# Transposing the seven MLP input forms on the way into DRAM instead of on the way out

## The chip, the cores and the metric

The kernel runs one layer of a streaming encoder on one core of a Trainium2 chip. The metric is device microseconds (us) of that core, from one launch. Five engines work side by side, each through its own instruction stream in order: TensorE (PE in the profile; its weight loads are PEld), VectorE (DVE), ScalarE (ACT), GpSimd (POOL) and SyncE (SP). SP does no arithmetic here: it issues DMAs, and so does POOL. A DMA that an engine issues waits in that engine's stream until its data are ready, and what stands behind it waits too. Engines signal each other by semaphores.

## The reference, cut to what matters

One layer, 2048 frames of 1024 features, everything in float32:

```
h = layer_norm(ALPHA * h + mix, ln1_g, ln1_b)        # mix: mLSTM and gated linear attention heads
xa = memory_cross_attention(h, mem, x_wq, x_wk, x_wv, x_wo)
h = layer_norm(ALPHA * h + xa, ln2_g, ln2_b)
ff = squared_relu_mlp(h, w_ff1, w_ff2)               # square(relu(h @ w_ff1)) @ w_ff2, width 4096
h = layer_norm(ALPHA * h + ff, ln3_g, ln3_b)
```

The kernel keeps float32 accuracy by splitting each factor into a high and a low float16 half, and multiplying high by high, high by low and low by high (`mm3`, lines 167 to 172).

## The kernel before, in words

The kernel has three stages. Stage A (to about 1130 us of the span) computes the mixer. Stage B (about 1130 to 1730 us) goes over 16 tiles of 128 frames with three steps that are staggered in one loop: in its turn i it runs `s1(i)` (output projection of the mixer and the first layer norm, LN1), `s2(i-1)` (attention scores and softmax) and `s3(i-2)` (attention output and the second layer norm, LN2). Stage C (to the end) is the MLP.

TensorE multiplies along the partition axis, so every left operand must stand transposed. Stage B has that done by transposing DMAs that SP issues (`to_T`, line 222): for each tile, the mixer's output `y_d` into `whi`, LN1's output into `wlo` (`h1T` in the code) and the softmax into `pT`. `pT` has one buffer, so tile i's transpose waits until `s3(i-1)` has read the last one.

The MLP's first product uses a fast matrix scheme with 7 products in place of 8: two neighbouring tiles and the two halves of the features make a 2x2 block of the input, and 7 combinations of its four parts (the forms, 128x512 each) are multiplied by 7 combinations of the weights. The forms of a pair are made at the end of `s3(i)` for odd i (i is then the pair's second tile; lines 978 to 998): GpSimd and VectorE make the sums, and four turns of a loop make the halves of forms k = 0 and 1, of 2, of 3 and 4, and of 5 and 6 in a tile `hs3` (two buffers; `hs` in the profile). A turn's ACT copy makes the high half, its DVE subtraction the low half, and GpSimd stores the result to `h2_d`, one DRAM tile per pair (`h_d` in the profile, which leaves numbers out of names; the other `h_d` that is loaded into `r` is the mixer's residual). Then the tile itself is scaled and stored (`ah_d`).

The MLP goes over the frames in two halves of 8 tiles, and in each half over 16 weight groups. Stage C needs form f of a half as one tile [128, 4 pairs, 2, 4, 128], transposed: `c_form` reads it from `h2_d` by four transposing DMAs of 256 KB, one per pair. For the first half, SP issues 7x4 of them at turn 16 of stage B, as soon as the memory of LN1's weights is free; the first product block, `ffn1(0, 0)`, stands between `s3(14)` and `s3(15)` on TensorE. For the second half they are issued in the last weight group of the first half. `ffn1(j, half)` has 7 products of 12 matmuls, in the order A11, S2, S3, S1, A12, S4, A22, into two banks of each of two PSUM names (`mm`, `o`); ACT copies A11 out, DVE adds the others up.

The tiles `whi` and `wlo` of pool `wsp` have four buffers each. Weights pass through them in stages A and C, `h1T` in stage B.

What sets the order: within an engine, a scheduler orders the instructions of stages A and B before the run, by its own model of durations, and the chip keeps that order; in stage C most of it is in the order of the code. Two instructions of POOL matter below. The power of LN1 and LN2 (`L202`, 1/sqrt by `pow`) is on the way of every layer norm. And between a `partition_all_reduce` (`L130`) and the next ordinary instruction POOL loads other code, and again on the way back.

Of the kernel before, what the change touches and what calls it, by code (L numbers as in the profile page):

```python
# [10 lines left out]
F16 = mybir.dt.float16  # L11
# [6 lines left out]
P = 128  # L18
T = 2048
D = 1024  # L20
KC = D // P
NT = T // P
# [37 lines left out]
def layer_kernel(ctx: ExitStack, tc, a, out):  # L60
    nc = tc.nc
# [5 lines left out]
    wsp = ctx.enter_context(tc.tile_pool(name="wsp", bufs=4))  # L67
    big = ctx.enter_context(tc.tile_pool(name="big", bufs=4))
    ps = ctx.enter_context(tc.tile_pool(name="ps", bufs=1, space=PSUM))
    dram = ctx.enter_context(tc.tile_pool(name="dram", bufs=1, space=bass.MemoryType.DRAM))  # L70
# [4 lines left out]
    def ps_s():  # L75
        return ps.tile([P, 512], F32, name="s", bufs=4)
# [4 lines left out]
    def slab(shape, dt):  # L81
        return big.tile(shape, dt, name="slab")
# [6 lines left out]
    h0_d = [dram.tile([P, D], F32, name=f"h0_d{i}") for i in range(NT)]  # L89
    ah2_d = [dram.tile([P, D], F32, name=f"ah2_d{i}") for i in range(NT)]  # L90
    y_d = [dram.tile([CPB, P, 8, 2, P], F16, name=f"y_d{b}") for b in range(NB)]
    h2_d = [dram.tile([P, 7, D], F16, name=f"h2_d{i}") for i in range(NT // 2)]
    w1_d = [dram.tile([4, P, 2048], F16, name=f"w1_d{j}") for j in range(NJ)]
    w2_d = [dram.tile([2, P, 2048], F16, name=f"w2_d{j}") for j in range(NJ)]
    nm_d = dram.tile([64, P], F32, name="nm_d")
# [71 lines left out]
    def mm3(psum, pairs, start=True, stop=True):  # L167
        n = len(pairs)
        for i, (lh, ll, rh, rl) in enumerate(pairs):
            nc.tensor.matmul(psum, lhsT=lh, rhs=rh, start=(start and i == 0), stop=False)  # L170
            nc.tensor.matmul(psum, lhsT=lh, rhs=rl, start=False, stop=False)  # L171
            nc.tensor.matmul(psum, lhsT=ll, rhs=rh, start=False, stop=(stop and i == n - 1))  # L172
# [21 lines left out]
    def layer_norm(x, gt, bt, spread=False):  # L194
        st = sm.tile([P, 2, 6], F32, name="st")
        mv = sm.tile([P, 2], F32, name="mv")
        rs = sm.tile([P, 2], F32, name="rs")
        for i in range(2):
            nc.vector.bn_stats(st[:, i, :], x[:, i * 512:(i + 1) * 512])  # L199
        nc.vector.bn_aggr(mv, st.rearrange("p a b -> p (a b)"))  # L200
        nc.vector.tensor_scalar(rs[:, 0:1], mv[:, 1:2], EPS, None, ALU.add)
        nc.gpsimd.tensor_tensor(rs[:, 1:2], rs[:, 0:1], mhalf[:, 0:1], ALU.pow)  # L202
        if spread:
            nm = sm.tile([P, 1], F32, name="amx")
            nc.vector.scalar_tensor_tensor(nm, mv[:, 0:1], -1.0, rs[:, 1:2], ALU.mult, ALU.mult)
            nc.scalar.activation(x, x, AF.Identity, scale=rs[:, 1:2], bias=nm)
            nc.gpsimd.tensor_tensor(x, x, gt, ALU.mult)
            nc.gpsimd.tensor_tensor(x, x, bt, ALU.add)
            return
        nc.vector.scalar_tensor_tensor(x, x, mv[:, 0:1], gt, ALU.subtract, ALU.mult)  # L210
        nc.vector.scalar_tensor_tensor(x, x, rs[:, 1:2], bt, ALU.mult, ALU.add)
# [9 lines left out]
    def to_T(dst, src):  # L221
        nc.sync.dma_start_transpose(dst, src)  # L222
# [696 lines left out]
    with ExitStack() as bctx:  # L919
# [45 lines left out]
        def s3(i):  # L965
            r, pT = rs_.pop(i)[0], es_.pop(i)
            for n in range(2):
                ns = slice(n * 512, (n + 1) * 512)
                po = ps_s()
                mm3(po, [(pT[:, 0, f * P:(f + 1) * P], pT[:, 1, f * P:(f + 1) * P], vo[f // 2][0][:, f % 2, ns],  # L970
                          vo[f // 2][1][:, f % 2, ns]) for f in range(8)])
                nc.vector.scalar_tensor_tensor(r[:, ns], po, inv_o, r[:, ns], ALU.mult, ALU.add)
            layer_norm(r, g2, b2)
            if i % 2 == 0:
                even[0] = r
                return
            r0, r1 = even[0], r
            if i < NT - 1:
                fm = wst.tile([P, 2048], F32, name="stg")
                fm = fm[:, 0:D], fm[:, D:2 * D]  # L980
            else:
                fm = [rr.tile([P, D], F32, name="r") for _ in range(2)]
            t1, t2, t3, t4 = (f[:, k * 512:(k + 1) * 512] for f in fm for k in range(2))
            a0, a1, c0, c1_ = r0[:, 0:512], r0[:, 512:D], r1[:, 0:512], r1[:, 512:D]
            nc.gpsimd.tensor_tensor(t1, c0, a0, ALU.subtract)
            nc.gpsimd.tensor_tensor(t3, c1_, c0, ALU.subtract)
            nc.vector.tensor_tensor(t2, c1_, t1, ALU.subtract)
            nc.vector.tensor_tensor(t4, a1, t2, ALU.subtract)
            for k, src in ((0, r0), (2, c1_), (3, fm[0]), (5, fm[1])):
                n = src.shape[-1] // 512  # L990
                hs = bx.tile([P, 2, 2, 512], F16, name="hs3", bufs=2)[:, 0:n]
                src = src.rearrange("p (n c) -> p n c", n=n)
                nc.scalar.copy(hs[:, :, 0], src)
                nc.vector.tensor_tensor(hs[:, :, 1], src, hs[:, :, 0], ALU.subtract)
                nc.gpsimd.dma_start(h2_d[i // 2][:, k:k + n], hs.rearrange("p n s c -> p n (s c)"))
            for ii, rx in ((i - 1, r0), (i, r1)):
                nc.scalar.activation(rx, rx, AF.Copy, scale=ai_h2)
                nc.gpsimd.dma_start(ah2_d[ii], rx)
# [5 lines left out]
        ORDER = (0, 4, 5, 3, 1, 2, 6)  # L1004

        def c_form(t, half, f):
            for p in range(4):
                to_T(t[:, p].rearrange("p s k t -> p (s k) t"), h2_d[half * 4 + p][:, f])
            forms[half, f] = t

        def form_tile(pool, name):
# [169 lines left out]
        for i in range(2, NT + 2):  # L1181
            if i < NT:
                s1(i, bx)
            if i == NT:
                b2ctx.close()
                c1 = c1ctx.enter_context(tc.tile_pool(name="c1", bufs=1, reuse_waits="tile", side="right"))
                for f in ORDER[:5]:
                    c_form(form_tile(c1, f"hf{f}"), 0, f)
# [4 lines left out]
            if i == NT:  # L1193
                za, zb = slab([P, 4096], F32), slab([P, 4096], F32)
                stgs[1] = za[:, 0:2048]
                zt += [za[:, 2048 + k * 512:2560 + k * 512] for k in range(4)]
                for n, f in enumerate(ORDER[5:]):
                    c_form(form_stage(zb[:, n * 2048:(n + 1) * 2048]), 0, f)
                w1_load(1)
# [3 lines left out]
            if i == NT + 1:  # L1203
                mx_0 = ffn1(0, 0, {})
            s3(i - 2)
            if i == NT - 2:
                stgs[0] = wst.tile([P, 2048], F32, name="stg")
                w1_new(0)
                w1_load(0)
                t = w1_tasks(0, stgs[0])  # L1210
# [4 lines left out]
    with ExitStack() as cctx:  # L1215
# [3 lines left out]
        for n in range(2):  # L1219
            t = slab([P, 4, D], F32)  # L1220
# [63 lines left out]
        with tc.manual_schedule():  # L1284
# [17 lines left out]
            n = 0  # L1302
            slots = None
            for half in range(2):
                for j in range(NJ):
# [4 lines left out]
                    if half == 0:  # L1310
                        w2t[j] = [w2s[n % 2][:, k] for k in range(2)]
                        t2 = w2_tasks(j)
                        if j + 1 < NJ:
                            w1_new(j + 1)
                            t1 = w1_tasks(j + 1, stgs[1])
                            t1["bound"]()
                            t1["scale"]()
                            ta = t20 if j == 1 else t2
                            ex = {0: [t1["split_a"], t1["split_b"], ta["bound"]],
                                  1: [t1["sums_a"], ta["scale"], t1["sums_b"], t1["split_s"]],  # L1320
                                  2: [lambda: t1["split_l"](0)], 3: [ta["split"]],
                                  4: [lambda: t1["split_l"](1)]}
                            if j == 1:
                                ex[3].append(u0[5])
                        else:
                            w1_reload(0)
                            slots = [forms[0, f] for f in ORDER[:4]]
                            slots = [spare, form_stage(stgs[1]), slots[0], form_stage(stgs[0])] + slots[1:]
                            ex = {0: [lambda: c_form(slots[1], 1, ORDER[1]), t2["bound"], t2["scale"]],
                                  1: [t2["split"], lambda: c_form(slots[2], 1, ORDER[2])]}  # L1330
                            for k in range(3, 7):
                                ex[k - 1] = [lambda k=k: c_form(slots[k], 1, ORDER[k])]
# [38 lines left out]
                    if half == 0 and j == NJ - 1:  # L1371
                        accs[:] = [*accs[8:10]]
                        for f in ORDER[4:]:
                            t = forms[0, f].rearrange("p i s k t -> p (i s k t)").bitcast(F32)
# [87 lines left out]
```

## Time and profile before

| what | value |
|---|---|
| median of 3 runs | 3002.34 us (3002.3 to 3006.09) |
| the profiled execution | 3002.87 us, of which the span is 3001.0 us |
| granted TensorE clock, mean | 0.951 |
| busy, share of the span | PE 91%, DVE 66%, ACT 37%, POOL 15% |
| transposing DMAs that read the forms back | 56, of 256 KB each |

A row of the timeline gives start, duration and engine of an instruction, its line, operation and tiles, and in brackets how long the engine was idle before it and what ended that. PE's durations overlap, since matmuls are pipelined: neighbouring 512-column matmuls start 0.22 us apart at the full clock (1.0, 2.4 GHz) and 0.43 us apart at half of it. SPq and POOLq rows are DMA issues, and last as long as the issue, not the transfer.

### The profile page before, as it was taken

The page shows a single profiled execution, that of the slowest core. Times are in us where ns is not written, and L with a number is a line of the kernel's source. Part 1 is how long each engine was busy: PE and PEld are TensorE (multiplying, and loading weights), DVE is VectorE, ACT ScalarE, POOL GpSimd, SP SyncE. Part 2 cuts the span into 40 slices and gives each one's busy share as a digit, 9 for nine tenths or more (in the row PEclk, how much of TensorE's full clock was granted, in tenths as well). Part 3 has the DMA queues.
Part 4 walks back from the last instruction along what each step waited for, and adds up shares of the span by engine and source line. Part 5 has one row for each costly group of instructions (what it writes and reads, how often), then busy time and mean ns, then how long its engine had stood idle before and what let it go on. Part 6 is the DMA issues. An engine that isn't in the chain of part 4 may idle for free.

```text
span 3001.0 us, 41124 instructions
## 1 busy us (share of the span) xinstructions
PE 2738.2 (91%) x16282; PEld 1545.8 (52%) x16282; DVE 1991.3 (66%) x3774; ACT 1096.3 (37%) x1715; POOL 447.6 (15%) x573
## 2 busy tenths in 40 slices
PE   3679989989998898999999779999999999999997
PEld 2346667666665665565565334444444444444443
DVE  8956774655768666676666467777776676555547
ACT  3335444434444543233223254444443222222230
POOL 1102113322433221121111110000000000000003
PEclk8789999988989999999999889999999999999999
DMA  7832331010001335344435963333345522122211
GB/s 240 240 118 86 106 97 38 20 42 9 23 26 62 98 120 128 66 133 106 109 102 134 175 216 142 134 134 134 134 146 141 194 90 109 67 77 78 78 53 57
DMA packets 276993, 319.51 MB, mean 106 GB/s; under 512 B 200944, under 2 KB 217856, under 8 KB 268096
## 3 DMA queue, kind: packets, MB, share of 16 engines
q1 hardware_dynamic: 268096, 285.43, 31.3%
q0 software_dynamic: 8704, 31.46, 2.9%
q8 instruction: 127, 2.08, 0.3%
q14 instruction: 66, 0.54, 0.1%
HBM read 165.58 MB, written 102.96 MB: 89 GB/s over the span
## 4 chain that ended last, share of the span: by engine, by line
PE 67%; DVE 15%; issue 7%; POOL 4%; ACT 3%; DMA 2%; SPq 2%; POOLq 0%; ACTq 0%; DVEq 0%
PE s L170 9%; PE s L171 9%; PE s L172 9%; PE mm L170 9%; PE mm L172 8%; PE mm L171 8%; PE o L172 4%; PE o L170 4%; PE o L171 4%; SPq L222 2%; DVE wmx L114 1%; DVE qk L334 1%; DVE wlo L148 1%; DVE st L199 1%; PE o L651 1%
## 5 line engine op out<-in xcount | busy, mean ns | idle before, releaser
L1245 DVE SCALAR_TENSOR_TENSOR slab<-s,uiv,slab 128x512 f32<-128x512 f32 x384 | 285.5, 748 | 99.0 <-PE s L172 97.5
L170 PE MATMUL mm<-whi,slab 128*128 128x256 f16 x1024 | 280.3, 274 | 12.4 <-ACT whi L147 7.2
L171 PEld LDWEIGHTS <-whi 128*128 128x128 f16 x1680 | 167.1, 99 | 238.8 <-issue 70.6
L171 PE MATMUL mm<-wlo,slab 128*128 128x256 f16 x1024 | 280.3, 274 | 2.7 <-DVE wlo L148 2.7
L172 PE MATMUL mm<-whi,slab 128*128 128x256 f16 x1024 | 280.3, 274 | 0.0
L172 PEld LDWEIGHTS <-wlo 128*128 128x128 f16 x1936 | 191.9, 99 | 168.4 <-issue 12.6
L170 PEld LDWEIGHTS <-whi 128*128 128x128 f16 x1680 | 167.0, 99 | 198.0 <-issue 13.8
L171 PE MATMUL s<-w,ua 128*128 128x512 f16 x512 | 194.0, 379 | 1.8 <-DVE w L148 1.8
L170 PE MATMUL s<-w,ua 128*128 128x512 f16 x512 | 194.0, 379 | 0.0
L172 PE MATMUL s<-w,ua 128*128 128x512 f16 x512 | 194.0, 379 | 0.0
L172 PE MATMUL o<-slab,wlo 128*128 128x256 f16 (+1 forms) x640 | 189.1, 295 | 0.0
L170 PE MATMUL s<-w,ub 128*128 128x512 f16 x480 | 182.6, 380 | 2.9 <-DVE r L1245 2.9
L171 PE MATMUL s<-w,ub 128*128 128x512 f16 x480 | 182.6, 380 | 0.0
L172 PE MATMUL s<-w,ub 128*128 128x512 f16 x480 | 182.4, 380 | 0.0
L170 PE MATMUL mm<-slab,whi 128*128 128x512 f16 x448 | 178.4, 398 | 0.4 <-ACT sg L343 0.4
L171 PE MATMUL mm<-slab,whi 128*128 128x512 f16 x448 | 178.4, 398 | 0.0
L172 PE MATMUL mm<-slab,wlo 128*128 128x512 f16 x448 | 178.1, 397 | 0.0
L170 PE MATMUL mm<-hf,whi 128*128 128x512 f16 x384 | 146.4, 381 | 11.5 <-ACT slab L1142 11.5
L171 PE MATMUL mm<-hf,whi 128*128 128x512 f16 x384 | 146.3, 381 | 0.0
L172 PE MATMUL mm<-hf,wlo 128*128 128x512 f16 x384 | 146.3, 381 | 0.0
L170 PEld LDWEIGHTS <-slab 128*128 128x128 f16 x1104 | 109.3, 99 | 64.8 <-issue 23.2
L170 PE MATMUL o<-slab,wlo 128*128 128x256 f16 x512 | 139.7, 273 | 0.0
(423 smaller groups left out, 6296.8 us busy)
## 6 DMA issues: line engine op xcount, KB each, us to landing
stg<-in_w_ff SPq DMA_DIRECT2D x17, 1024.0 KB
w_d<-w SPq DMA_DIRECT2D x32, 512.0 KB
slab<-in_w_ff SPq DMA_DIRECT2D x15, 1024.0 KB
w<-w_d SPq DMA_DIRECT2D x30, 512.0 KB
stg<-in_w_x SPq DMA_DIRECT2D x14, 1024.0 KB
stg<-in_w_mix SPq DMA_DIRECT2D x14, 1024.0 KB
h_d<-hs POOLq DMA_DIRECT2D x24, 512.0 KB, 3.8
x<-in_x SPq DMA_DIRECT2D x16, 512.0 KB
```

Of the source, the lines that this page charges most:

```text
L114: nc.vector.tensor_reduce(dst, src, axis=AX.X, op=ALU.max, apply_absolute_value=True)
L148: nc.vector.scalar_tensor_tensor(lo, stg, s, hi, ALU.mult, ALU.subtract)
L170: nc.tensor.matmul(psum, lhsT=lh, rhs=rh, start=(start and i == 0), stop=False)
L171: nc.tensor.matmul(psum, lhsT=lh, rhs=rl, start=False, stop=False)
L172: nc.tensor.matmul(psum, lhsT=ll, rhs=rh, start=False, stop=(stop and i == n - 1))
L199: nc.vector.bn_stats(st[:, i, :], x[:, i * 512:(i + 1) * 512])
L222: nc.sync.dma_start_transpose(dst, src)
L334: nc.vector.scalar_tensor_tensor(cv, raw[:, t:t + TB], cj[:, t:t + 1], cv, ALU.mult, ALU.add)
L651: nc.tensor.matmul(po[j][:, c], lhsT=ATb[j][:, c], rhs=vs[j][:, c], start=True, stop=(S is None))
L1245: nc.vector.scalar_tensor_tensor(acc[ii][:, ns], po, iv, acc[ii][:, ns], ALU.mult, ALU.add)
```

## The change

The four turns of the loop now transpose `hs3` by a DMA from SBUF to SBUF (SP) into a tile `ht` of pool `wsp`, under the name `wlo`, and GpSimd stores each transposed form from there to a DRAM tile per half and form. `c_form` becomes one plain DMA of 1 MB. Line numbers after line 995 rise by 4 and then fall by 1.

```diff
-    h2_d = [dram.tile([P, 7, D], F16, name=f"h2_d{i}") for i in range(NT // 2)]
+    h2_d = [[dram.tile([P, 4, 2, 4, P], F16, name=f"h2_d{h}{f}") for f in range(7)] for h in range(2)]
...
                 nc.vector.tensor_tensor(hs[:, :, 1], src, hs[:, :, 0], ALU.subtract)
-                nc.gpsimd.dma_start(h2_d[i // 2][:, k:k + n], hs.rearrange("p n s c -> p n (s c)"))
+                ht = wsp.tile([P, 2048], F16, name="wlo")[:, 0:n * D]
+                to_T(ht.rearrange("p (b t) -> p b t", t=P), hs.rearrange("p n s c -> p (n s c)"))
+                ht = ht.rearrange("p (n s k t) -> p n s k t", n=n, s=2, k=4)
+                for m in range(n):
+                    nc.gpsimd.dma_start(h2_d[i // 8][k + m][:, i % 8 // 2], ht[:, m])
...
         def c_form(t, half, f):
-            for p in range(4):
-                to_T(t[:, p].rearrange("p s k t -> p (s k) t"), h2_d[half * 4 + p][:, f])
+            nc.sync.dma_start(t, h2_d[half][f])
             forms[half, f] = t
```

On SP, in the regular part of stage B, before (`whi<-y_d` is the mixer's output for the next `s1`, `wlo<-whi` is `h1T`):

```order
L222 DMA_TRANSPOSE whi<-y_d_115 128x16x128
L222 DMA_TRANSPOSE wlo<-whi 128x16x128
L222 DMA_TRANSPOSE pT<-hs_13572 128x16x128
L222 DMA_TRANSPOSE whi<-y_d_116 128x16x128
L222 DMA_TRANSPOSE wlo<-whi 128x16x128
```

And now, at the same place (`wlo<-hs` are the new transposes, 128x8x128 the one of form 2 alone):

```order
L222 DMA_TRANSPOSE wlo<-whi 128x16x128
L222 DMA_TRANSPOSE wlo<-hs_13945 128x16x128
L222 DMA_TRANSPOSE pT<-hs_13867 128x16x128
L222 DMA_TRANSPOSE wlo<-hs_13952 128x8x128
L222 DMA_TRANSPOSE wlo<-hs_13958 128x16x128
L222 DMA_TRANSPOSE wlo<-hs_13965 128x16x128
L222 DMA_TRANSPOSE whi<-y_d_116 128x16x128
L222 DMA_TRANSPOSE wlo<-whi 128x16x128
```

The transpose of forms 0 and 1 stands behind `h1T`, those of the other forms between `pT` and the next load from `y_d`.

On POOL, the end of a pair's forms and LN1 of the next tile, before (`ah_d<-r` is the scaled tile, `r<-h_d` a residual for a later `s1`):

```order
L202 TENSOR_TENSOR rs<-rs,mhalf 128x1 x2
L985 TENSOR_TENSOR stg<-r 128x512
L986 TENSOR_TENSOR stg<-r 128x512
L995 DMA h_d_119<-hs_13362 128x1024
L998 DMA ah_d_101<-r 128x1024
L995 DMA h_d_119<-hs_13366 128x2048
L998 DMA ah_d_100<-r 128x1024
L995 DMA h_d_119<-hs_13370 128x2048
L202 TENSOR_TENSOR rs<-rs,mhalf 128x1
L811 DMA r<-h_d_90 128x1024
L811 DMA r<-h_d_91 128x1024
```

And now:

```order
L985 TENSOR_TENSOR stg<-r 128x512
L986 TENSOR_TENSOR stg<-r 128x512
L1002 DMA ah_d_101<-r 128x1024
L999 DMA h_d_120<-wlo 128x1024
L1002 DMA ah_d_100<-r 128x1024
L999 DMA h_d_121<-wlo 128x1024
L999 DMA h_d_122<-wlo 128x1024
L811 DMA r<-h_d_90 128x1024
L999 DMA h_d_123<-wlo 128x1024
L999 DMA h_d_124<-wlo 128x1024
L202 TENSOR_TENSOR rs<-rs,mhalf 128x1
L811 DMA r<-h_d_91 128x1024
```

The same LN1 power now stands behind five stores of transposed tiles, and one load of `r` ahead of it and one behind it.

On DVE, at the start of stage C, before: the splitting and summing of weight group 1 (`L148 wlo`, `L1057`, `L1058`) lies among LN2 of tile 14 and the first sums of `ffn1(0, 0)` (`L1144`):

```order
L972 SCALAR_TENSOR_TENSOR r<-s,inv_o,r 128x512
L148 SCALAR_TENSOR_TENSOR wlo<-slab,w_s,whi 128x1024
L199 BN_STATS st<-r 128x6
L148 SCALAR_TENSOR_TENSOR wlo<-slab,w_s,whi 128x512
L200 BN_AGGR mv<-st 128x2
L1057 TENSOR_TENSOR slab<-slab 128x512
L201 TENSOR_SCALAR rs<-mv 128x1
L210 SCALAR_TENSOR_TENSOR r<-r,mv,g_12105 128x1024
L1058 TENSOR_TENSOR slab<-slab 128x512
L1144 TENSOR_TENSOR slab<-o,slab 128x512
```

And now (`L987` to `L994` are the forms of tiles 14 and 15, `umx` is the first instruction for the scale of `ffn1(0, 0)`'s result):

```order
L211 SCALAR_TENSOR_TENSOR r<-r,rs,b_12112 128x1024
L987 TENSOR_TENSOR r<-r 128x512
L994 TENSOR_TENSOR hs_16678<-r,hs_16678 128x512
L988 TENSOR_TENSOR r<-r 128x512
L994 TENSOR_TENSOR hs_16684<-r,hs_16684 128x2x512
L994 TENSOR_TENSOR hs_16691<-r,hs_16691 128x2x512
L148 SCALAR_TENSOR_TENSOR wlo<-slab,w_s,whi 128x1024
L148 SCALAR_TENSOR_TENSOR wlo<-slab,w_s,whi 128x512
L1060 TENSOR_TENSOR slab<-slab 128x512
L1061 TENSOR_TENSOR slab<-slab 128x512
L1072 SCALAR_TENSOR_TENSOR wlo<-slab,w_s,whi 128x1024 x2
L1172 TENSOR_REDUCE umx<-zmx 128x1
```

The work on weight group 1 and that scale now come after LN2 and all forms of tile 15.

## Rows read from the trace of the kernel before

**Rows 1.** The page, part 1: busy time, share, instructions
```profile
PE 2738.2 (91%) x16282; PEld 1545.8 (52%) x16282; DVE 1991.3 (66%) x3774; ACT 1096.3 (37%) x1715; POOL 447.6 (15%) x573
```

**Rows 2.** Stretches: length; PE, PEld, DVE, ACT, POOL busy; clock, DMA share, GB/s
```profile
1395.00:1460.00 65.00, 63.05 (x386) 37.52 (x385) 43.84 (x69) 20.20 (x36) 12.82 (x14) 1.00 0.42 110
...
1622.40:1732.25 109.85, 85.25 (x470) 46.67 (x468) 55.10 (x90) 30.90 (x53) 12.52 (x15) 0.89 0.80 162
1732.25:1762.81 30.56, 15.17 (x61) 6.23 (x60) 16.27 (x25) 13.37 (x16) 6.34 (x9) 0.76 0.78 299
...
1675.00:1700.00 25.00, 11.62 (x43) 4.78 (x44) 3.40 (x8) 1.71 (x4) 0.00 (x0) 0.63 1.12 163
...
1775.00:1800.00 25.00, 25.00 (x118) 11.29 (x116) 21.13 (x42) 14.63 (x23) 1.42 (x3) 1.00 0.59 211
...
2309.00:2337.00 28.00, 28.00 (x132) 12.70 (x130) 18.19 (x31) 8.38 (x17) 0.35 (x1) 1.00 0.99 190
```

**Rows 3.** Timeline of SP: DMA issues
```profile
1415.53 2.47 SPq L222 DMA_TRANSPOSE wlo<-whi  x1
...
1646.92 21.60 SPq L222 DMA_TRANSPOSE hf<-h_d  x15
1668.62 6.22 SPq L222 DMA_TRANSPOSE pT<-hs  x1
...
1687.67 11.94 SPq L222 DMA_TRANSPOSE slab<-h_d  x8
```

**Rows 4.** Timeline of PE
```profile
1431.21 0.38 PE L170 MATMUL mm<-wo_h,whi 128*128 128x512 f16 x1
...
1688.38 0.61 PE L170 MATMUL s<-slab,pT 128*128 128x512 f16 x1 [19.95 <-DMA pT<-hs]
...
1754.10 0.58 PE L170 MATMUL mm<-hf,whi 128*128 128x512 f16 x1 [11.49 <-ACT slab L1142]
...
1762.81 0.58 PE L170 MATMUL o<-slab,whi 128*128 128x512 f16 x1 [3.90 <-DVE slab L1144]
```

**Rows 5.** Timeline of DVE in a pair of stage B, and at the boundary
```profile
1406.33 1.23 DVE L994 TENSOR_TENSOR hs<-stg,hs 128x1024 f16<-128x1024 f32 x1 [0.15 <-issue]
...
1427.39 0.75 DVE L972 SCALAR_TENSOR_TENSOR r<-s,inv_o,r 128x512 f32<-128x512 f32 x1 [2.94 <-PE s L172]
...
1430.41 0.74 DVE L818 SCALAR_TENSOR_TENSOR r<-mm,inv_m,r 128x512 f32<-128x512 f32 x1
...
1748.91 1.22 DVE L994 TENSOR_TENSOR hs<-r,hs 128x1024 f16<-128x1024 f32 x1 [2.95 <-ACT hs L993]
```

**Rows 6.** Timeline of POOL
```profile
1407.85 0.53 POOL L995 DMA_DIRECT2D h_d<-hs  x1 [1.93 <-DVE hs L994]
1410.38 1.46 POOL L202 TENSOR_TENSOR rs<-rs,mhalf 128x1 f32<-128x1 f32 x1 [2.00 <-DVE rs L201]
...
1666.85 0.61 POOL L995 DMA_DIRECT2D h_d<-hs  x1 [1.45 <-DVE hs L994]
...
1750.43 0.53 POOL L995 DMA_DIRECT2D h_d<-hs  x1 [2.79 <-DVE hs L994]
1758.20 0.41 POOL L130 PARTITION_ALL_REDUCE amx<-wmx  x1 [7.25 <-issue]
```

**Rows 7.** DMA from 1400 to 1425: slices of 0.625 us, queues, one issue
```profile
GB/s 6 0 0 0 0 0 256 164 138 393 328 406 393 413 393 334 413 144 0 26 33 79 347 406 413 360 78 199 211 222 165 3 0 0 0 0 0 0 0 0
...
q0 software_dynamic: 944, 3.41, 36.2%
q1 hardware_dynamic: 2101, 0.53, 12.0%
...
h_d<-hs POOLq DMA_DIRECT2D x1, 256.0 KB, 2.4
```

**Rows 8.** Timeline of ACT at the boundary
```profile
1670.45 1.04 ACT L993 CAST hs<-stg 128x1024 f16<-128x1024 f32 x1 [0.62 <-DMA h_d<-hs]
```

**Rows 9.** PE's waits from 1120 to 1640: in total, times, longest
```profile
PE mm L170 <- DVE r L818: 23.2, 10, 6.8
```

## The prediction

> **What bounds the kernel now.** I read the busy shares first, then the stretches, then the timelines. TensorE (PE) is busy for 2738.2 us, 91% [rows 1], so a cost counts only where PE comes to wait for it. The stretches [rows 2] show where. One regular pair of stage B takes 65.00 us with PE busy for 63.05, so PE waits for about 2 us. From the start of the last pair (1622.40) to the end of its `s3` (1732.25) PE is busy for 85.25 of 109.85, at a mean clock of 0.89 (of 2.4 GHz); from there to the first product of `ffn1(1, 0)` that waits (1762.81) for 15.17 of 30.56. At 1775 to 1800 it is full, and so it is at 2309 to 2337, although DMA is at 0.99 there: that is where the 28 transposes of the second half run, and PE doesn't wait for them.
>
> The holes at the boundary are named on two engines. On SP [rows 3] 15 transposes into `hf` take 21.60 us to issue, only then does `pT` of tile 14 go out, at 1668.62, and behind it eight into a `slab`. On PE [rows 4] 19.95 us of idle time end at 1688.38 with just that `pT`, 11.49 at 1754.10 and 3.90 at 1762.81. From 1675 to 1700 the DMA share is 1.12 at 163 GB/s and the granted clock 0.63 [rows 2], so part of the loss is a cold clock behind the idle time.
>
> **What a transfer costs.** The only transposed 512 KB from 1400 to 1425 (q1, 0.53 MB) takes 12.0% of 25 us, 3.0 us of all 16 engines; the plain transfers of POOL's queue take 36.2%, 9.05 us, for 3.41 MB, 1.39 us per 512 KB and 2.8 per MB [rows 7]. A transposition with the engines to itself lands 3.9 us after its issue: issued at 1415.53 [rows 3], its last busy slice ends at 1419.4 [rows 7].
>
> The Trainium skill ("Advanced Engine Details and Errata", section "X-Bar Transpose (TRN2)") says that transposing transfers run as fast as regular ones. This trace disagrees: 3.0 us against 1.39, a factor of 2.2 [rows 7]. By the page the new transposes would take half as long in the queue, which would favour the first rival below and its 2991.
>
> **Second half's loads.** 28 transposes become seven loads at 2309 to 2337. PE is full there before, so this is 0 us.
>
> **Steady pairs: the added work.** Per pair SP gets four transposes more (1.75 MB, 3.5 × 3.0 = 10.5 us of the engines), and POOL issues seven stores instead of four. The transpose of forms 0 and 1 and the later load of `whi` from `y_d` have over 9 us until their `s1` by my reading of the order; I cost them at 0. The stores are another matter. LN1's power (L202) on POOL runs now from 1410.38 to 1411.84, waiting for DVE alone [rows 6]. After the change it stands in POOL's program behind the stores of form 5, which wait for their transposition, which waits for `hs`; that ends on DVE at 1406.33 + 1.23 = 1407.56 [rows 5]. So POOL is held, and behind the power wait LN1's result, `s1`'s input and DVE's next sums. The delay isn't in the trace, and I bound it from both sides.
>
> - Low: the transposition runs alone, 1407.6 + 3.9 = 1411.5; two stores at 0.53 of issue [rows 6], then 1.46 of power: 1414.0, 2.2 late.
> - High: everything queued at 1405 goes first. On SP's queue forms 3 and 4, and 5 and 6, 6.0; on POOL's two scaled tiles 2.8, a store of form 2 0.7, two of forms 3 and 4 1.4, a load of `r` 1.4, 6.3. So 1405.0 + 12.3 + 0.3 = 1417.6 for landing, and 1420.1 for the power: 8.3 late.
> - Taken: the two queues share the engines equally. The first transposition then takes twice its 3.0, to 1411; the second 3.0 and beside it the stores of forms 3 and 4, 1.4, to 1415.4; with 1.06 and 1.46 the power ends at 1417.9, 6.1 late. What speaks for sharing is the nearest saturated stretch: a store issued at 1666.85 released ACT at 1670.45, after 3.6 us [rows 6, 8], against 2.4 for the same 256 KB in the regular part [rows 7].
>
> How much of 6.1 comes to PE? DVE has 2.94 us idle ahead of L972 at 1427.39, ended by PE [rows 5]: that much of a delay of DVE is absorbed. Behind it there is nothing: L818 ends at 1430.41 + 0.74 = 1431.15 and PE takes the freed PSUM bank at 1431.21 [rows 4, 5]. PE waits for DVE's L818 ten times already between 1120 and 1640, 23.2 us in all [rows 9]. So a pair loses 6.1 − 2.94 = 3.15, and six pairs (odd tiles 1 to 11; the seventh, at tile 13, belongs to the boundary) lose 18.9. The bounds give 0 and 6 × (8.3 − 2.94) = 32.
>
> **Boundary, up to the end of `s3` of tile 15.** Now 109.85 − 85.25 = 24.6 us idle [rows 2], and some 2.5 by the cold clock (11.62 us busy at 0.63 [rows 2], with a little of the same kind on either side), 27.1. Afterwards the forms come by seven loads, 7 × 2.8 = 19.5 us of the engines, and `pT` of tile 14 doesn't stand behind 15 transposes: it is there about 2 us before PE wants it. What stays by the order: DVE does 28 instructions of `ffn1(0, 0)` between the sums of `s1` of tile 15 and the L818 that frees the banks, 3.5 us of idle time, and 1 in `ffn1(0, 0)` itself. Gain 27.1 − 4.5 = 22.6.
>
> **Boundary, from there to `ffn1(1, 0)`.** Now 30.56 us. Two things come later. The order shows that DVE splits and sums weight group 1, and begins the scale of `ffn1(0, 0)`'s result, only after the forms of tile 15. And the last forms go through a transposition and a store that stand behind eight loads of 1 MB; the last `hs` is ready on DVE at 1748.91 + 1.22, 17.9 after the end of `s3` [rows 5], so its last store goes out about 21.5 after. On POOL 7.25 us without a reason named lie between the last ordinary work and the all-reduce at 1758.20 [rows 6]; that stretch comes again, now behind the last store. Then follow the all-reduce, the scale, the split of `u`, the bound and a PSUM copy: 18 us from the last store to PE's product, estimated from the present order of these steps (1750.43 [rows 6] to 1762.81 [rows 4] is 12.4, with one all-reduce done earlier that is now late). So 21.5 + 18 = 39.5, a loss of 9 to 10. Net of the boundary −13, with bounds of −20 (the loads and scale fit where they are now) and −5 (the `c_acc` loads delay the last store by as much again).
>
> **Sum.** The profiled execution took 3002.87, 0.5 above the median. 3002.87 − 13 + 18.9 = 3008.8, rounded to 3009.
>
> **The rivals.**
> 1. The transpositions find the engines nearly free: the DMA share of a pair is only 0.42 [rows 2]. The power is then 2.2 to 2.9 late, DVE's 2.94 absorb it, steady loss 0 to 4, and the boundary gives 14 to 20. About 3002.9 − 14 + 2 = 2991 (2983 to 2997). For it: the mean share. Against it: the forms come in the busiest part of a pair (slices near 400 GB/s [rows 7]).
> 2. POOL's queue becomes the bound of a pair. If the power is 8.3 late or more, each pair loses over 5, six pairs 32, and the loads of `r` behind the stores press on `s1` as well; the boundary gives 5 to 10. 3002.9 + 30 − 9 = 3024. It decides from the point where a transposition takes over 10 us from `hs` to landing. Slower. For it: the 1.12 share and 163 GB/s where many transposes are on the way [rows 2]; against it: there 15 were queued, here two.
> 3. The transfers weren't the limit at the boundary: what PE waited for there is replaced by DVE, whose work on weight group 1 and the scale has moved behind tile 15. The gain of 22.6 goes to that chain, the steady pairs hide theirs: 3003. Against it: 19.95 us were ended by `pT` itself [rows 4].
>
> **How the numbers follow.** Forecast 0.45, rival 1 0.30, rival 2 0.18, rival 3 0.07. No change means within 0.2%, 6 us: 2996.3 to 3008.3, about what a measurement can tell. The forecast's own range is 2998 to 3018: 0.21 slower, 0.21 same, 0.03 faster. Rival 1: 0.27 faster, 0.03 same. Rival 2: 0.18 slower. Rival 3: 0.05 same, 0.01 either side. Together 0.31 faster, 0.29 same, 0.40 slower. For 8 in 10 the range runs from 2985 to 3022: it leaves out the lower edge of rival 1 and the upper half of rival 2.
>
> **What would show it.** In a regular pair, POOL's power L202 stands behind the two stores of form 5 and 6 and ends some 6 us later than in [rows 6]; PE's waits for DVE's L818 rise from 10 to about 16 times and by some 19 us. The wait of 19.95 for `pT` is gone. Between the end of `s3` of tile 15 and the first product of `ffn1(1, 0)` PE idles for more than now, about 40 us in all, the all-reduce again behind 7 us of nothing. At the half's change nothing differs. The prediction is wrong if L202 isn't late (rival 1), if pairs take more than 70 us (rival 2), or if the boundary gains over 20 or nothing.

## The result, and the profile after

The changed kernel took 3052.03 us (median of 4 runs, 3044.62 to 3062.98), the kernel before 3004.08 (4 runs): a ratio of 1.0162, 95% interval 1.0128 to 1.0197. It is slower by 48 us; 3009 was predicted, and the range ended at 3022. The profiled execution's span is 3042.9 against 3001.0, so 41.9 us more have to be found.

TensorE runs the same 16282 products and is busy for 10.7 us more (page, part 1; it answers to [rows 1]): of the 41.9 us, 31.2 are waiting and 10.7 are products that ran slower, at a colder clock.

```profile
PE 2748.9 (90%) x16282; PEld 1547.5 (51%) x16282; DVE 1993.4 (66%) x3774; ACT 1095.9 (36%) x1715; POOL 456.3 (15%) x597
```

To place them I use one mark, the second `L972` of each odd tile, which ends that tile's `s3`. It cuts the time from stage B on into four parts. DVE's timeline after, at tiles 13 and 15:

```profile
1700.18 0.75 DVE L972 SCALAR_TENSOR_TENSOR r<-s,inv_o,r 128x512 f32<-128x512 f32 x1 [3.70 <-PE s L172]
...
1755.52 0.75 DVE L972 SCALAR_TENSOR_TENSOR r<-s,inv_o,r 128x512 f32<-128x512 f32 x1 [3.70 <-PE s L172]
```

and before:

```profile
1657.99 0.75 DVE L972 SCALAR_TENSOR_TENSOR r<-s,inv_o,r 128x512 f32<-128x512 f32 x1 [3.70 <-PE s L172]
...
1733.20 0.73 DVE L972 SCALAR_TENSOR_TENSOR r<-s,inv_o,r 128x512 f32<-128x512 f32 x1
```

From tile 13 to tile 15, with the loads of the forms in between, the time fell from 75.2 to 55.3 us. By the same marks (times between them, in us; tail is what is left of the span; the last column is from the mark of tile 15 to the first product with `ua` on PE; `ua` holds the halves of the result of `ffn1(0, 0)`, so this is the first of the MLP's second products):

| kernel (profiled run) | five pairs, tiles 1 to 11 | sixth, 11 to 13 | boundary, 13 to 15 | tail | to `ua` |
|---|---|---|---|---|---|
| before | 325.1 | 69.1 | 75.2 | 1267.8 | 37.6 |
| after | 365.7 | 75.0 | 55.3 | 1287.4 | 53.2 |
| difference | +40.6 | +5.9 | -19.9 | +19.6 | +15.6 |

These sum to 46.2; the stages ahead of tile 1's mark were 4.4 shorter in the profile of after, which gives 41.8. Over the profiles of all runs below that mark lies anywhere from 1253.8 to 1272.4, so I take the 4.4 for scatter; that is not shown.

**A pair.** Stretches of after (columns as in [rows 2], which has 65.00 us and 63.05 of PE for a pair). The first row is a whole pair, the second and third lie in it, the fourth is the tail up to `ua`, the fifth lies in the half's change:

```profile
1332.05:1406.34 74.29, 67.41 (x386) 38.67 (x384) 43.79 (x68) 20.10 (x36) 13.56 (x17) 0.93 0.55 121
1341.00:1348.00 7.00, 4.99 (x19) 2.05 (x18) 5.62 (x8) 3.45 (x4) 1.65 (x3) 0.76 0.84 204
1371.25:1380.00 8.75, 3.88 (x13) 1.66 (x12) 7.66 (x12) 1.04 (x1) 1.52 (x1) 0.71 0.59 120
1756.27:1808.72 52.45, 25.04 (x82) 9.46 (x83) 28.31 (x47) 19.74 (x20) 9.44 (x13) 0.71 0.70 220
2300.00:2400.00 100.00, 100.00 (x465) 45.31 (x463) 59.80 (x103) 35.42 (x59) 1.79 (x4) 1.00 0.57 221
```

The pair's PE is busy for 67.41 with as many products: 4.4 us more, at a colder clock (0.93 over the pair), and idle for 6.9, 4.9 more. Over the five pairs it is 14.0 us more of PE time and 26.6 more of waiting. PE's waits show the place:

```profile
1343.29 0.38 PE L170 MATMUL mm<-wo_h,whi 128*128 128x512 f16 x1 [2.01 <-DVE r L818]
...
1344.98 0.63 PE L170 MATMUL mm<-wo_h,whi 128*128 128x512 f16 x1
...
1376.12 0.58 PE L170 MATMUL mm<-wo_h,whi 128*128 128x512 f16 x1 [4.87 <-DVE r L818]
```

The wait of 2.01 was there before (1.95); that of 4.87 is new. In total, PE's waits for L818 from 1120 to 1640 are now (total, times, longest; [rows 9] had 23.2 in 10):

```profile
PE mm L170 <- DVE r L818: 47.2, 13, 7.5
```

DVE waited for POOL once and for ACT twice. From the third of these rows on it is idle for 0.62 us in one place and for a few hundredths elsewhere, up to the end of the `L818` that PE waits for:

```profile
1357.15 1.28 DVE L211 SCALAR_TENSOR_TENSOR r<-r,rs,b 128x1024 f32<-128x1024 f32 x1 [4.65 <-POOL rs L202]
...
1364.06 1.22 DVE L219 TENSOR_TENSOR whi<-r,whi 128x1024 f16<-128x1024 f32 x1 [5.56 <-ACT whi L218]
...
1368.33 0.18 DVE L956 RECIPROCAL r<-sum 128x4 f32<-128x4 f32 x1 [2.25 <-ACT e L953]
...
1375.33 0.75 DVE L818 SCALAR_TENSOR_TENSOR r<-mm,inv_m,r 128x512 f32<-128x512 f32 x1
```

POOL after:

```profile
1351.74 1.07 POOL L999 DMA_DIRECT2D h_d<-wlo  x2 [6.16 <-DMA wlo<-hs]
1352.80 0.55 POOL L811 DMA_DIRECT2D r<-h_d  x1
1355.46 1.07 POOL L999 DMA_DIRECT2D h_d<-wlo  x2 [2.11 <-DMA wlo<-hs]
1356.54 0.57 POOL L202 TENSOR_TENSOR rs<-rs,mhalf 128x1 f32<-128x1 f32 x1
```

LN1's power ends 25.0 us after the pair's mark; in [rows 6] 1411.84 is 18.0 after the mark at 1393.8. It is held by 7.0, as the prediction had it (6.1). ACT after:

```profile
1361.94 1.15 ACT L812 ACTIVATE r<-r,h_a 128x1024 f32<-128x1024 f32 x1 [16.90 <-DMA r<-h_d]
1363.00 1.03 ACT L218 CAST whi<-r 128x1024 f16<-128x1024 f32 x1
1363.94 0.56 ACT L953 ACTIVATE e<-o,nb,c 128x256 f32<-128x256 f32 x1
...
1368.10 0.20 ACT L953 ACTIVATION_READ_ACCUMULATOR e<-o,nb,c 128x1 f32 x1
```

Here is what the prediction didn't have. ACT stands for 16.90 us (13.6 to 17.4 over the five pairs) at the scaling of `r` (L812), whose load POOL issued at 1352.80, 9.1 us earlier. LN1's cast and the softmax's exponentials stand behind it in ACT's program. LN1's result had been there since 1358.4. Before, the first scaling stood behind LN1's cast and the first two exponentials, and ACT waited 0.69 for its load; the scheduler has moved it ahead of the cast. ACT before:

```profile
1413.20 1.04 ACT L218 CAST whi<-r 128x1024 f16<-128x1024 f32 x1 [6.96 <-DVE r L211]
...
1416.03 1.15 ACT L812 ACTIVATE r<-r,h_a 128x1024 f32<-128x1024 f32 x1 [0.69 <-DMA r<-h_d]
```

The loads of `r` themselves have become slower: from issue to landing 8.2 us after (first fence), 4.6 before (second, the same part of a pair):

```profile
r<-h_d POOLq DMA_DIRECT2D x2, 512.0 KB, 8.2
```

```profile
r<-h_d POOLq DMA_DIRECT2D x2, 512.0 KB, 4.6
```

**The sixth pair.** No `r` is loaded or scaled in it, so its 5.9 us have another cause. DVE waits there for an all-reduce of POOL, for 5.49 us ahead of the end of the softmax (3.47 before). The all-reduce comes 31.0 us after the mark, behind the last two stores; before it came at 24.7. In e4, e8 and e11 below, whose sixth pair has the old stores, it comes at 25.0 to 25.2, and the pair takes 69.5 to 69.9. No run moves it alone, and in e1, where POOL has none of these stores, it still comes at 30.4: that it costs the 5.9 is read from the traces, not tested.

**The tail.** PE after, behind `s3` of tile 15:

```profile
1770.87 0.61 PE L172 MATMUL mm<-hf,wlo 128*128 128x512 f16 x1 [14.96 <-DVE wlo L148]
...
1796.98 0.59 PE L170 MATMUL mm<-hf,whi 128*128 128x512 f16 x1 [7.70 <-ACT slab L1145]
```

The first is the splitting of weight group 1, which DVE does behind the forms. On DVE and POOL:

```profile
1777.82 2.48 DVE L1072 SCALAR_TENSOR_TENSOR wlo<-slab,w_s,whi 128x1024 f16<-128x1024 f32 x2 [3.44 <-DMA h_d<-wlo]
```

```profile
1781.27 1.07 POOL L999 DMA_DIRECT2D h_d<-wlo  x2 [1.83 <-DMA wlo<-hs]
1790.95 0.41 POOL L130 PARTITION_ALL_REDUCE amx<-umx  x1 [8.61 <-issue]
```

The weights wait for a `wlo` buffer until a form's store has landed, and the all-reduce comes 8.61 after the last store's issue, much as in [rows 6] (7.25).

### The profile page after: what moved, and what is told of

Same layout as the page of the kernel before. It is cut to its first block, busy times and chain, and to the rows that moved or that the text cites. A ratio compares the mean times of both kernels' runs of the same rounds, so it can differ in the third digit from the quotient of the medians.

```text
span 3042.9 us, 41156 instructions
## 1 busy us (share of the span) xinstructions
PE 2748.9 (90%) x16282; PEld 1547.5 (51%) x16282; DVE 1993.4 (66%) x3774; ACT 1095.9 (36%) x1715; POOL 456.3 (15%) x597
## 5 line engine op out<-in xcount | busy, mean ns | idle before, releaser
L170 PEld LDWEIGHTS <-whi 128*128 128x128 f16 x1680 | 168.3, 100 | 202.0 <-issue 17.4
L170 PE MATMUL mm<-wo_h,whi 128*128 128x512 f16 x256 | 105.4, 412 | 58.6 <-DVE r L818 54.3
```

## The experiments

Two theories for the pairs. **A** (also A1), the prediction's: the power held on POOL. **R** (A2 in e3): ACT, which waits for `r`. A third, **C** or **T**: the transposes in themselves. All figures beside "before" come from the same chip as the run. Times of a pair and of points in it are read from the timelines, counted from the mark that opens the pair; the five pairs of the table are meant.

**e1, stores by SP.**

```diff
-                    nc.gpsimd.dma_start(h2_d[i // 8][k + m][:, i % 8 // 2], ht[:, m])
+                    nc.sync.dma_start(h2_d[i // 8][k + m][:, i % 8 // 2], ht[:, m])
```

> The changed kernel with one edit: the seven stores per pair of transposed forms are issued by SP and no longer by POOL. Theory A (POOL is held: LN1's power and the loads of r stand behind stores that wait for their transposition): the power follows its variance within 2.5 us again, PE's wait for L818 in the even tile's s1 goes from 4.9 back to under 1, a pair takes 65 to 66.5 us, and behind s3 of tile 15 the all-reduce of umx no longer follows the last store; the whole falls from 3052 to 2990 to 3005. Theory C (the transposes themselves, their traffic and their use of the wlo buffers, cost it): a pair stays at 72 to 74 us, the whole at 3040 or more.

3011.01 (before 3000.93; ratio 1.0031, 1.0014 to 1.0048). Pairs of 65.0 to 66.8; the power at 19.9. Theory C seems to fall: all the new transposes are still there. The whole came out above what was expected: the tail kept most of its loss (1282.8) and the sixth pair all of it (75.0).

**e2, the transposes alone.** In the kernel before, behind each store of `hs3`:

```diff
+                ht = wsp.tile([P, 2048], F16, name="wlo")[:, 0:n * D]
+                to_T(ht.rearrange("p (b t) -> p b t", t=P), hs.rearrange("p n s c -> p (n s c)"))
```

> The kernel before with the change's transposes added: every hs3 is also transposed into a wlo tile which nothing reads; the forms are stored untransposed by POOL and loaded by transposing DMAs as before. Theory A: nothing on POOL waits for a transposition, so pairs take 65 to 66.5 us and the whole 3004 to 3012. Theory C: pairs take 70 to 74 and the whole is 3035 to 3055, since the boundary keeps its old holes too.

3076.87 (ratio 1.0254, 1.0226 to 1.0282), the slowest of all. Pairs of 72.2 to 76.1, although the power is only 2 late (20.2 to 20.7). By what was expected, that is for C and against A, and e1 against C: neither stands as put. ACT in the pair that begins at 1404.6:

```profile
1428.08 0.19 ACT L953 ACTIVATION_READ_ACCUMULATOR e<-o,nb,c 128x1 f32 x1
1436.28 1.15 ACT L812 ACTIVATE r<-r,h_a 128x1024 f32<-128x1024 f32 x1 [8.01 <-DMA r<-h_d]
```

ACT waits between the two halves of the softmax for `r`, whose loads land after 11.2 us here:

```profile
r<-h_d POOLq DMA_DIRECT2D x2, 512.0 KB, 11.2
```

With untransposed stores beside them the three transposes also hold SP for 15.39 us (10.82 in the change), and PE waits 1.4 to 5.1 for the next `whi` behind them.

**e3, the loads of r by SP,** in the changed kernel:

```diff
-            nc.gpsimd.dma_start(r, h0_d[i])
+            nc.sync.dma_start(r, h0_d[i])
```

> The changed kernel with one edit: the loads of r (L811) go by SP, behind the transposes of the forms, and not by POOL. Theory A1 (the power alone): the power is still 6 us late, PE still waits 3 us or more in the even tile's s1, a pair takes 69 to 72. Theory A2 (ACT waits for a load of r that POOL issues late, with LN1's cast behind it): ACT's wait of 16.9 for r is gone and a pair takes under 68, the whole 3020 or less. If SP's queue delivers r no earlier, nothing changes: 3045 to 3060.

3009.03 (ratio 1.003, 1.0016 to 1.0043), 43 less than the change. Pairs of 65.3 to 67.0. ACT's wait is down to 0.8 to 3.6:

```profile
1418.33 1.15 ACT L812 ACTIVATE r<-r,h_a 128x1024 f32<-128x1024 f32 x1 [3.63 <-DMA r<-h_d]
```

But it doesn't tell A1 from R: without the loads the scheduler put the power ahead of the last two stores, so it was late by only 0.7 to 3.3:

```profile
1409.53 1.07 POOL L999 DMA_DIRECT2D h_d<-wlo  x2 [3.56 <-DMA wlo<-hs]
1410.62 0.57 POOL L202 TENSOR_TENSOR rs<-rs,mhalf 128x1 f32<-128x1 f32 x1
1417.80 1.12 POOL L999 DMA_DIRECT2D h_d<-wlo  x2 [6.60 <-DMA wlo<-hs]
```

**e4, the change for the first half alone** (`if i // 8 == 0`, otherwise stores and loads as before).

> The change for the first half of the frames alone (pairs 0 to 3): pairs 4 to 7 are stored untransposed and loaded by transposing DMAs, as in the kernel before. The boundary gets its plain loads, the tail behind s3 of tile 15 has no new transposes. By the account from the traces (pairs lose about 8 us each, the boundary gives 20, the tail loses 20): 4 x 8 - 20 + 0 = +12 against before, 3016 (3008 to 3024), with pairs 4 to 6 at 65 us and from s3 of tile 15 to full PE as before. If the tail's loss comes from DVE's order and not from transposes and stores, it stays: 3035.

3012.28 (ratio 1.0039, 1.0021 to 1.0058), as expected from the account. The four pairs with transposes take 71.4 to 75.1, the fifth 65.0, the sixth 69.5, the boundary 51.0, the tail 1269.2. So the tail's loss, and the 5.9 of the sixth pair, come with the second half's forms.

**e5, e2 with the loads of r by SP.** (The edit of e3 in the kernel of e2.)

> The kernel of e2 (the kernel before, with transposes that nothing reads) with one edit: the loads of r go by SP, behind the transposes of the forms. In e2 a pair takes 72 to 76 us, nothing on POOL waits for a transposition, and ACT waits 8.0 us between the two halves of a softmax for a load of r that takes 11.2 us to land. Theory R (that load of r is what the pairs lose by): ACT's wait falls to 4 or less, pairs take 65 to 67.5, the whole falls by 40 to 55 to 3020 to 3037, and the tail's loss of 20 stays. Theory T (the transposes slow pairs in another way, such as the load of whi or the two hs3 buffers): pairs stay at 70 or more, the whole at 3055 or more.

3062.55 (ratio 1.0208, 1.0173 to 1.0244); pairs of 71.2 to 72.0. My expectation for R failed and the figures for T came out. SP's timeline says why R's did not: the loads now stand behind transposes that hold SP for 16.55 (2.5 of it between their issues).

```profile
1405.76 16.55 SPq L222 DMA_TRANSPOSE wlo<-hs  x3
1422.40 1.01 SPq L811 DMA_DIRECT2D r<-h_d  x2
```

```profile
1426.35 1.15 ACT L812 ACTIVATE r<-r,h_a 128x1024 f32<-128x1024 f32 x1 [5.69 <-DMA r<-h_d]
```

`r` is still late, and the power is not (20.0 to 20.2). The edit didn't bring `r` early; it speaks neither way on whether early is enough. In e2 and e5 the transposes are there and the pairs slow, in e1 and e3 they are there and the pairs fast; so a pair is not slow by the transposes in themselves, but by what they make late.

**e6, the power held, without transposes:** the kernel before, `r` by SP, and nine powers for one in the LN1 that stands behind a pair's forms.

```diff
+        for _ in range(hold[0]):
             nc.gpsimd.tensor_tensor(rs[:, 1:2], rs[:, 0:1], mhalf[:, 0:1], ALU.pow)
```

> The kernel before with the loads of r on SP and the LN1 power of tiles 4, 6, 8, 10, 12 and 14, the ones behind a pair's forms, repeated nine times on POOL (eight more of 0.57 to 1.46 us, so 5 to 12 late). No transposes are added. This prices the prediction's own term. Theory A1 (the prediction's: what the power is late by, less 2.94, is lost by PE): at 5 to 6 late 2 to 3 us of wait in each held pair and 3 to 5 with the colder clock, so 3015 to 3035 in all; more in proportion if the delay is longer. If ACT's order and DVE's other work hide it: pairs stay at 65 to 66 and the whole at 3000 to 3007.

3003.38 (ratio 1.0005, 0.9991 to 1.0019): nothing. The power ends at 22.9 to 24.1, 5 to 6 late, while `r` is early (issued by 16.8 after the mark), and the five pairs take 327.1 together (before 325.1). Four take 65.1; the fifth takes 66.7 with the same single wait of 1.95, its products at a mean clock of 0.97.

```profile
1409.48 6.42 POOL L204 TENSOR_TENSOR rs<-rs,mhalf 128x1 f32<-128x1 f32 x9 [2.00 <-DVE rs L202]
```

**e9, ACT doesn't wait for r.** The changed kernel without the scaling of `r`, so that the residual is added as it is; this also saves ACT 1.15 us of work a tile. POOL's order is as in the change.

```diff
-            nc.scalar.activation(r, r, AF.Copy, scale=ai_h0)
```

> The changed kernel with one thing left out: ACT's scaling of r behind its load (L812), so that the residual is added unscaled. POOL's program is the same, word for word: LN1's power still stands behind the stores of forms 5 and 6, the loads of r still between and behind the stores. Only ACT no longer waits for r; DVE needs it first at its L818. Theory R (ACT waits for r in front of LN1's cast and of the softmax): the softmax's second exponentials end by 30 us after the pair's start and not after 36, pairs go from 72 to 75 back to 65 to 67.5, the whole to 2998 to 3014. Theory A1 (the power held on POOL): pairs stay at 69 or more, the whole at 3030 or more.

3020.75 (before 3002.15; ratio 1.007, 1.0047 to 1.0093), 31 less than the change. The whole lies between the two expectations (up to 3014 for R, from 3030 for A1): the sixth pair (74.4) and the tail (1289.4) kept their losses. Pairs of 66.4 to 68.0, one of five above the 67.5 of R. The power is nearly as late as in the change, at 23.7 to 25.3:

```profile
1353.04 1.07 POOL L998 DMA_DIRECT2D h_d<-wlo  x2 [1.93 <-DMA wlo<-hs]
1354.13 0.57 POOL L202 TENSOR_TENSOR rs<-rs,mhalf 128x1 f32<-128x1 f32 x1
```

and the pair (its mark is at 1329.7) has its PE time and clock back:

```profile
1329.70:1396.10 66.40, 63.09 (x386) 37.56 (x384) 43.73 (x69) 18.12 (x34) 13.59 (x17) 1.00 0.58 135
```

The pairs tell the two apart. Of the 40.6 us that the five pairs lost, 31.1 go when ACT's wait for `r` goes (334.6 against 365.7); the 9.5 that stay, 1.9 a pair (4.5 of them waiting, 5.0 colder clock), are all that the held power and the rest can claim.

The runs together, sorted by the end of the softmax's last exponentials on ACT (us after the mark):

| kernel | power ends | exponentials end | pair |
|---|---|---|---|
| before | 18.0 | 26.5 to 26.9 | 65.0 |
| e1 | 19.9 to 20.0 | 28.7 to 29.2 | 65.0 to 66.8 |
| e6 | 22.9 to 24.1 | 29.6 to 30.8 | 65.1 to 66.7 |
| e3 | 18.7 to 21.3 | 29.8 to 31.0 | 65.3 to 67.0 |
| e9 | 23.7 to 25.3 | 29.6 to 31.3 | 66.4 to 68.0 |
| e5 | 20.0 to 20.2 | 33.0 to 34.1 | 71.2 to 72.0 |
| after | 25.0 to 25.2 | 33.9 to 36.6 | 71.9 to 74.9 |
| e2 | 20.2 to 20.7 | 36.0 to 39.2 | 72.2 to 76.1 |

The pair's length follows the third column and not the second. Up to some 30 us (3 to 4 late) a delay costs PE at most 0.6 us of waiting for L818, which fits the 2.94 that DVE has idle in [rows 5]: 26.6 and 2.94 are 29.5. The pairs of 66.7 and 66.8 in e1, e3 and e6 have no added wait (PE is idle for 1.95 to 2.01); the clock fell in them. Past 30 us a pair loses more than what the delay exceeds the slack by, since the clock falls behind the wait: the first pair after is 8.6 late, 5.7 past the slack, and lost 7.7.

**The tail: e7 and e10.** e7 is e3 with the last pair's forms in the free buffers of `e`:

```diff
-                ht = wsp.tile([P, 2048], F16, name="wlo")[:, 0:n * D]
+                ht = (bx.tile([P, 4, NMEM], F32, name="e", bufs=2).rearrange("p h m -> p (h m)").bitcast(F16) if i == NT - 1 else wsp.tile([P, 2048], F16, name="wlo"))[:, 0:n * D]
```

> The kernel of e3 (the change with the loads of r on SP) with one edit: the forms of the last pair (tile 15) are transposed into the free buffers of the softmax tile e and not into wlo. Theory W (in the tail the weights of group 1 wait for wlo buffers that the forms hold, and DVE's order follows from that): from s3 of tile 15 to the first product with ua PE loses no 14.9 us for wlo any more, the stretch falls from about 50 to under 36 us, and the whole from 3009 to 2988 to 2996, below the kernel before. Theory X (the traffic of the last transposes delays the weights' loads and SP): the stretch stays over 45, the whole at 3005 or more.

3008.4 (before 3001.15; ratio 1.0027, 1.0015 to 1.004), the same as e3 and not the 2988 to 2996 of W. The wait for `wlo` is gone, and DVE does weight group 1 ahead of tile 15's `s3`; yet 53.1 us to `ua` stay, since two other waits came up:

```profile
1744.56 0.58 PE L170 MATMUL mm<-hf,whi 128*128 128x512 f16 x1 [15.39 <-ACT slab L1145]
...
1764.31 0.58 PE L170 MATMUL o<-slab,whi 128*128 128x512 f16 x1 [15.46 <-DVE slab L1147]
```

The second leads back to POOL, whose all-reduce stands behind the last stores:

```profile
1752.03 1.07 POOL L999 DMA_DIRECT2D h_d<-e  x2 [5.98 <-DMA e<-hs]
1759.70 0.41 POOL L130 PARTITION_ALL_REDUCE amx<-wmx  x1 [6.60 <-issue]
```

e10 is e7 with the last pair's stores by SP.

> The kernel of e7 (r on SP, the last pair's forms in buffers of e) with one edit: the last pair's stores go by SP. In e7 the wait of 14.9 us for wlo was gone and two of 15.4 had come, the second for an all-reduce of POOL behind the last stores at 1752. If the two limits stand one behind the other (wlo's buffers, then POOL's stores), the stretch from s3 of tile 15 to the first product with ua now falls from 53 to 36 to 42 us and the whole from 3008 to 2990 to 2998. If a third one stands behind them (the traffic of the transposes), the stretch stays over 46.

3003.82 (ratio 1.0005, 0.9986 to 1.0023); 46.2 us to `ua`, and not 36 to 42. POOL was a limit, worth 7 us of that stretch by one profile of each, and not the last one: a wait of 15.61 for ACT's copy and one of 8.38 for DVE remain. What holds those I have not tried.

**The better version: e8 and e11.** e8 is e4 with the loads of `r` by SP, e11 is e8 with the transposed stores by SP too.

> The kernel of e4 (the change for the first half alone) with the loads of r on SP. Theory R: pairs 0 to 3 fall from 71 to 75 us to 65 to 67.5, the boundary keeps its gain of about 24 and the tail stays as before: 2978 to 2990, below the kernel before. If the loads of r are not the cause in this kernel: 3008 to 3016 as in e4.

> The kernel of e8 (change for the first half alone, loads of r on SP), with the stores of transposed forms by SP too: the candidate for the best version. In e1 most pairs took 65.0 us, in e8 65.6 to 66.8, so 0 to 5 us less than e8: 2976 to 2983. If SP's stores, which wait for their transposition, hold up the loads of r behind them on the same queue past 29 us after a pair's start, pairs go to 70 and the whole to 2995 or more.

e8: 2982.25 (before 3001.15; ratio 0.994, 0.992 to 0.9961). e11: 2980.28 (before 3002.15; ratio 0.9927, 0.9911 to 0.9943). Both beat the kernel before, within what was expected; between the two nothing is shown. In e11 the five pairs take 329.0, the boundary 51.3, the tail 1267.5. A pair with transposes and the tail up to `ua`:

```profile
1326.90:1392.30 65.40, 63.10 (x385) 37.55 (x384) 43.89 (x68) 20.32 (x36) 9.45 (x8) 1.00 0.62 137
1711.05:1748.48 37.43, 20.94 (x77) 8.34 (x76) 20.73 (x34) 17.74 (x19) 7.08 (x10) 0.73 0.62 238
```

The transposes are all there in the pair (DMA share 0.62 against 0.42 in [rows 2]), at 65.40. And a late `r` is harmless where nothing urgent stands behind it: in the four pairs of e11 with transposes the second scaling starts only 33.9 to 34.5 after the mark, but there the scheduler put it behind the exponentials, which end by 30.0.

## Why the prediction was wrong

**What held.** The boundary gave 19.9, predicted 22.6: the wait of 19.95 for `pT` [rows 4] is gone. (This counts the sixth pair's 5.9 among the pairs, as the prediction does. It falls on `s1(14)`, inside the stretch that the prediction took for the boundary; that stretch went from 111.0 to 96.9.) At the half's change PE is full, as forecast. POOL's power is held by the stores, 7.0 late where 6.1 was forecast. The tail lost for two of the reasons given: weight group 1 behind the forms, the all-reduce behind the last stores.

**The step that failed** is "So POOL is held, and behind the power wait LN1's result, `s1`'s input and DVE's next sums", which made the power the only way from the stores to PE. It was priced at 3.15 a pair, 18.9 for six; six pairs lost 46.5, the first five 8.1 each. e6 shows 5 to 6 us of held power to cost 0.1 to 1.7 a pair, e9 that in the change it and all else cost 1.9. The slack of 2.94 was read rightly, but the power's delay does not reach DVE whole: 5 to 6 us of it put the exponentials 3 later in e6 (4 in one pair), 5.7 to 7.3 put them 3 to 5 later in e9. The other 6.2 (31.1 over five pairs) come by the loads of `r`. I had one of them in the high bound as 1.4 us of traffic, and both in rival 2 as pressing "on `s1`"; neither asked who waits for them. ACT does. Any pair of ACT's timeline before would have shown that the softmax stands behind them: its order there is exponentials, `r`, `r`, exponentials; in the change LN1's cast stood behind the first as well. The load is issued 2.7 us later in its pair (20.7 after the mark against 18.0), and lands 9.1 us after its issue and not in some 4.6. In the sixth pair it was again not the power, but POOL's all-reduce behind the stores, as far as the traces show.

**A term left out** is the clock. The five pairs lost 14.0 us of PE time beside the 26.6 of waiting; at the boundary I had counted the cold clock, in the pairs not.

**A reading that was wrong** is the 3.9 us of a transposition "with the engines to itself" in the low bound: two loads of `r`, issued at 1411.80 and 1412.38, were on their way beside it (4.6 to landing).

**A term mis-sized** is the tail, +19.6 (15.6 of it up to `ua`) where 9 to 10 were forecast. The order had shown that weight group 1 comes late; it was priced as if only the all-reduce's chain decided. The `wlo` buffers that the forms share with the weights were not in the prediction at all, and by e7 they are what turned DVE's order round. That e4, e8 and e11 have the old tail shows that all of it hangs on the second half's forms, whose early transposition gains nothing, as the prediction said of the half's change.

**The rivals.** Rival 1 fell for the change, but what it pictured is what e8 and e11 reach, with half of the forms: transposes in the pairs at next to no cost, and the boundary's gain kept (2982 and 2980, against its 2991). Rival 2 named the right place, POOL's queue with the loads of `r`, and its sign, pairs over 70 us, came; its 3024 was 28 short, since it had 30 for the pairs, where 46.5 were lost, and 9 gained at the boundary net of the tail, where it was 0.3, and tied its point (10 us from `hs` to landing) to the power. The rule weighed in the prediction, that transposing transfers run as fast as regular ones (the Trainium skill, "Advanced Engine Details and Errata", "X-Bar Transpose (TRN2)"), does not fit the change's trace either: in the pair from 1332.09 to 1406.38 the 16 engines spent 40.2% of the time on 4.98 MB transposed and 14.9% on 3.93 MB plain, 6.0 and 2.8 us per MB, a factor of 2.1.

## What to carry to other kernels

When transfers are added to a busy stretch, go through every load that is issued on the same queue or lands in the same microseconds, and for each ask which in-order engine waits for it and what stands behind that wait; here a load that nobody hurried for stopped the softmax. A delay that one instruction's slack absorbs says nothing about the next: test the slack of each by delaying it alone. And do the part of a change that gains (the half on the path) without the part that gains nothing; here that, with the loads of `r` moved to another queue (e8), turned 1.6% slower into 0.6% faster.

## What the runs showed of the hardware

- Transposes and plain transfers side by side slow each other. Per MB the 16 engines spent 5.2 us on transposes and 2.6 on plain transfers over a pair of before (from its mark at 1393.83 to the next), 6.0 and 2.8 in the change, where most stores come after the transposes, and 6.3 and 3.6 in e2 (pair from 1404.57), where they run beside them. With the same transfers on POOL's queue, a 512 KB store landed after 3.6 us before and 7.7 in e2, a load of `r` after 4.6 and 11.2.
- Gaps of one length on PE were followed by either level of the clock: after 1.95 us idle in [rows 2]'s pair it stayed at 1.00 over the whole pair, and after 2.01 in the change the products went from 0.38 to 0.63 us (0.76 over 1341 to 1348, so at times 1.2 and not 2.4 GHz). In e1 a wait of 2.02 (at 1480) was followed by products of 0.38; in the fifth pair of e6 the wait of 1.95 was followed by products of 0.63. That fall cost e6's pair 1.7 us of PE time (64.76 for 63.10). Why the one fell and the others not is open.
